# Context steps of two scan directions on the two halves of TensorE's columns, and the running tile of a triangular inverse in PSUM

## The chip, the cores and the metric

The kernel runs on one core of one Trainium2 chip. The metric is the device time of one execution in microseconds, as the median of several runs. The core has TensorE (PE in the rows, with its weight loads as PEld), VectorE (DVE), ScalarE (ACT), GpSimd (POOL), the SyncE queue that issues transfers (SP), SBUF, and PSUM with eight banks of 512 float32 per partition.

## The reference, cut to what matters

The program is a two-layer backbone over 256 latent tokens behind 256 context tokens, 1024 features wide. Layer 0 mixes time with a bidirectional RWKV-7 scan over 16 heads of 64 and then runs a mixture of experts; layer 1 is a short convolution and a second mixture of experts. The change touches the scan alone:

```python
def step(s, inp):
    w_t, k_t, v_t, kk_t, a_t, r_t = inp
    sa = jnp.einsum('bhvk,bhk->bhv', s, -kk_t)
    s = (s * w_t[:, :, None, :] + sa[..., None] * (kk_t * a_t)[:, :, None, :]
         + v_t[..., None] * k_t[:, :, None, :])
    y = jnp.einsum('bhvk,bhk->bhv', s, r_t) if with_output else None
    return s, y
...
for p, reverse in enumerate((False, True)):
    ...
    s_ctx, yc = _wkv_scan(dec_c, kd_c, v_c, kk_c, a_c, None, s0, reverse)
    _, yl = _wkv_scan(dec_l, kd_l, v_l, kk_l, a_l, r_l, s_ctx, reverse)
```

For each of the two directions the state runs first through the context, where only the state counts, and then through the latent tokens, where each step gives an output too.

## The kernel before

The scan is done in chunks of 64 tokens: four context chunks (group g = 0) and four latent ones (g = 1). Two heads make a block of 128 features, and eight blocks (`fb` 0 to 7) pass through a software pipeline. For each block the kernel does the following.

- `first`, `second` and `pre` make the operands of the chunks for each direction d: decays, keys, and the products `pab`, `pat` and `pq` on TensorE, which ScalarE and VectorE take out of PSUM.
- `inverse` inverts the unit triangular 32x32 blocks of all chunks of both directions by forward substitution on VectorE. After the transpose `a_l` there are 31 steps; each is a product `lv` from `a_l` and a column of the running tile `t_l` (L820), and a subtraction that updates `t_l` (L822). Then `t_l` is transposed into `t_d` (L824). Before each inverse GpSimd clears `t_l` and writes its unit diagonal (L809 and two `pcopy`).
- `solve` (per direction) copies `t_d` into the block diagonal `d_bd` on ScalarE (L831) and does six products per group on TensorE (L843). Their banks are those of the pool `p2pq`, four of them, which `pre` uses too. ScalarE takes three of the results out (L853, L858, L862), VectorE subtracts the last two from `rd` and `hk` (L869, L872). Two banks stay open as accumulators for a whole direction.
- `chain` runs the state through the eight chunks. A step (i, d) is a product with `hk` and `v_bd` (L886) and one with `rd` and the state `s_bd` (L893) into one bank `po` of a pool of two. In a context step only 64 rows of it are made. Then VectorE copies one head's state (L896) and ScalarE the other's (L897) back to SBUF for the next step. Latent steps also give 64 rows of output, which ScalarE copies (L901) or VectorE adds (L903).
- `finish` normalizes and gates the block's output.

The generators are interleaved by `drive`, which always advances the one that has used the smallest share of its weight; a scheduler then sets the final order of each engine's queue, and each engine works through its queue strictly in that order. For each block there are two drives: the first holds `solve` of the current block, 22 steps of the next block's inverse, `finish` of the previous block and `first` of the block after; the second holds `chain` of the current block (weight 16), the remaining steps of the inverse (11) and `both` (weight 22), which makes the operands of the block after. The last block has no inverse beside it: its `chain` and `finish` run in a third drive with high priority (weight 19), beside the output projection `project` of the first seven blocks. Four tiles of the pool `p2pq` then become the projection's accumulators.

## Time and profile before

| | us |
|---|---|
| median of 3 runs | 1366.07 (1361.18 to 1366.48) |
| the profiled execution | 1364.24 |
| its span in the profile | 1362.4 |
| busy in the span: PE, DVE, ACT, POOL | 1196.9, 763.2, 582.8, 235.4 |
| inverse, products `lv` (L820) and updates of `t_l` (L822), 248 each | 81.7 and 78.9 |

The span begins with the first instruction and ends with the last. The scan's pipeline takes up the time from about 160 to 640 us. An engine's busy share is an average over the span, so it is read stretch by stretch: the transposes L813 (start of an inverse) and L824 (its end) mark the blocks. A duration in brackets at the end of a row of the timeline is the engine's idle time before the row, with what ended it.

### The profile page before, as it was taken

To read this page: it belongs to the slowest core of one execution; us is meant where nothing else is said; L and a number is where in the kernel's file an instruction comes from. 1 tells how busy PE (TensorE), PEld (TensorE's weight loads), DVE (VectorE), ACT (ScalarE), POOL (GpSimd) and SP (SyncE) were. 2 spreads that over 40 slices of the span, in tenths; PEclk is the share of its full clock that TensorE was granted. 3 is DMA by queue.
4 is the path that set the end of the run, shared out by engine and by line. 5 is a ranking of instruction groups with operands and counts; after the bars stand their busy time and mean duration, and the time that the engine had idled before them with its cause. 6 is when DMAs were issued, how large, how long until landed. Compare 5 with 4: busy or idle time off the path is not lost. (4 is left out here: it accounts for less than half of the span.)

```text
span 1362.4 us, 22076 instructions
## 1 busy us (share of the span) xinstructions
PE 1196.9 (88%) x8560; PEld 845.6 (62%) x8560; DVE 763.2 (56%) x1855; ACT 582.8 (43%) x1187; POOL 235.4 (17%) x245
## 2 busy tenths in 40 slices
PE   2799888889989888899789999889898799999797
PEld 2588687777867777788744444334898734444344
DVE  5878888889989998875532121211677512121112
ACT  4667562666756757744312122212644312112113
POOL 3313443332231232100200000000523200000001
PEclk9999999999999999999889999989999899999898
DMA  9455634133322320137679999978653399999860
GB/s 355 177 178 172 211 109 124 59 121 115 96 90 83 96 82 25 64 138 315 227 295 418 420 420 419 419 296 324 214 186 129 119 376 419 419 420 420 326 245 31
DMA packets 64630, 311.76 MB, mean 229 GB/s; under 512 B 14464, under 2 KB 22912, under 8 KB 29696
## 3 DMA queue, kind: packets, MB, share of 16 engines
q1 hardware_dynamic: 60192, 303.59, 58.0%
q10 hardware_dynamic: 4320, 6.63, 1.4%
q8 instruction: 71, 1.16, 0.3%
q14 instruction: 47, 0.39, 0.1%
HBM read 301.80 MB, written 8.39 MB: 228 GB/s over the span
## 5 line engine op out<-in xcount | busy, mean ns | idle before, releaser
L1558 PE MATMUL wup<-w,xe 128*64 128x512 f32 (+1 forms) x1024 | 261.5, 612 | 5.8 <-DVEq L1724 5.8
L1563 DVE TENSOR_TENSOR sgate<-sgate,wup 64x512 f32<-64x512 f32 (+1 forms) x32 | 22.1, 690 | 250.1 <-ACT sgate L1562 227.6
L1558 PEld LDWEIGHTS wup<-w,xe 128*64 128x64 f32 (+1 forms) x1024 | 77.4, 142 | 129.6 <-issue 120.4
L1585 PE MATMUL y<-w,het 128*64 128x512 f32 (+1 forms) x512 | 127.7, 598 | 0.0
L1597 DVE SCALAR_TENSOR_TENSOR yy<-y,gw,yy 64x512 fp32r<-64x512 f32 (+1 forms) x64 | 48.0, 750 | 121.3 <-ACT yy L1596 121.0
L1562 ACT ACTIVATE sgate<-wup 64x512 f32<-64x512 f32 (+1 forms) x32 | 19.0, 593 | 181.6 <-PE wup L1558 181.6
L1596 ACT ACTIVATE yy<-y,gw 64x512 fp32r<-64x512 f32 (+1 forms) x64 | 43.8, 684 | 122.0 <-PE y L1585 106.5
L820 DVE TENSOR_TENSOR lv<-a_l,t_l 128x126 f32<-128x126 f32 (+22 forms) x248 | 81.7, 330 | 3.3
L822 DVE TENSOR_TENSOR t_l<-t_l,lv 128x126 f32<-128x126 f32 (+22 forms) x248 | 78.9, 318 | 3.4
L886 PE MATMUL po<-v_bd,hk 128*64 128x128 f32 (+1 forms) x256 | 56.6, 304 | 21.1 <-ACT s_bd L897 7.5
L1585 PEld LDWEIGHTS y<-w,het 128*64 128x64 f32 (+1 forms) x512 | 37.6, 140 | 60.5 <-issue 57.2
L1510 PEld LDWEIGHTS xeps<-g,h2t 128*128 128x128 f32 x256 | 37.5, 216 | 38.2 <-issue 21.3
L1510 PE MATMUL xeps<-g,h2t 128*128 128x256 f32 (+1 forms) x256 | 45.8, 321 | 17.2 <-DVE gw L1498 10.7
L1105 ACT CAST wh<-w 128x1024 fp32r<-128x1024 f32 x40 | 41.7, 1046 | 41.4 <-PE dps L143 24.3
L1771 POOL TENSOR_SCALAR idrw<-cst 128x1024 f32<-128x1024 f32 x2 | 5.5, 2770 | 303.0 <-PE acc L1605 274.0
L886 PEld LDWEIGHTS po<-v_bd,hk 128*64 128x64 f32 (+1 forms) x256 | 31.7, 163 | 41.3 <-ACT s_bd L897 14.4
L144 PE MATMUL dps<-xh,wl 128*128 128x258 f32 x192 | 55.2, 288 | 2.1 <-POOL wl L1108 2.1
L142 PE MATMUL dps<-xh,wh 128*128 128x258 f32 x192 | 55.5, 289 | 1.5 <-ACT wh L1105 1.5
L766 PE MATMUL pab<-bk,al_bd 128*128 128x128 f32 x256 | 40.4, 306 | 18.1 <-DVE bk L744 13.7
L722 POOL TENSOR_TENSOR al_bd<-kkh,peb 64x512 f32<-64x512 f32 x32 | 39.8, 1245 | 90.9 <-ACT peb L713 89.0
L1605 PE MATMUL acc<-st,yy 128*128 128x256 f32 x272 | 46.5, 305 | 10.3 <-PEq L1724 9.4
L143 PE MATMUL dps<-xl,wh 128*128 128x258 f32 x192 | 55.2, 287 | 0.0
(414 smaller groups left out, 2938.4 us busy)
## 6 DMA issues: line engine op xcount, KB each, us to landing
w<-in_wgu SPq DMA_DIRECT2D x128, 1024.0 KB, 9.6
w<-in_wd SPq DMA_DIRECT2D x64, 1024.0 KB, 9.4
w<-in_ada SPq DMA_DIRECT2D x46, 1024.0 KB, 6.5
w<-in_sc_in SPq DMA_DIRECT2D x12, 1024.0 KB, 5.0
w<-in_rk SPq DMA_DIRECT2D x8, 1024.0 KB, 5.3
w<-in_wv SPq DMA_DIRECT2D x4, 1024.0 KB, 5.8
w<-in_wo SPq DMA_DIRECT2D x4, 1024.0 KB, 9.3
w<-in_sc_out SPq DMA_DIRECT2D x4, 1024.0 KB, 5.2
```

Of the source, the lines that this page charges most:

```text
L142: mm(out, lhs[0], rhs[0], start=start, stop=False)
L143: mm(out, lhs[0], rhs[1], start=False, stop=False)
L144: mm(out, lhs[1], rhs[0], start=False, stop=stop)
L820: nc.vector.tensor_mul(u, a_l[:, kk:kk + 1, kk + 1:].broadcast_to([P, m, n]), t_l[:, 0:m, kk:kk + 1].broadcast_to([P, m, n]))
L822: nc.vector.tensor_sub(t_l[:, 0:m, kk + 1:], t_l[:, 0:m, kk + 1:], u)
L886: nc.tensor.matmul(po[d][i], q.hk[d][g][:, j], q.vbd[:, 4 * g + j], start=True, stop=i == 0)
L1510: nc.tensor.matmul(pt[:, f * m:f * m + m], h2t[k][:, t, fb * P:fb * P + P], g[:, t, :, :n], start=j == 0, stop=j == 3)
L1558: nc.tensor.matmul(gu[i], x(kc), w[:, 512 * i:512 * i + 512], start=kc == 0, stop=kc == NB - 1)
L1585: nc.tensor.matmul(ys[i], het[:, k], w[:, 512 * i:512 * i + 512], start=k == 0, stop=k == 3)
L1596: nc.scalar.activation(parts[i][0], ys[i], AF.Copy, scale=gws[i])
L1597: nc.vector.scalar_tensor_tensor(parts[i][1], ys[i], gws[i], parts[i][0].bitcast(F32), op0=ALU.mult, op1=ALU.subtract)
L1605: nc.tensor.matmul(acc[4 * i + q], part[:, q * P:q * P + P], st, start=first and q % 2 + k == 0, stop=last and k == len(y) - 1, skip_group ...
```

## The change

It has two parts, and two weights follow.

The running tile `t_l` moves from SBUF to a PSUM bank of its own (pool `p2pt`), and the pool `p2pq` of the products goes from four banks to three. GpSimd can no longer set the tile up, so a template `t_0` is made once in SBUF, and ScalarE copies it to `t_l` before each inverse, after the four copies into `a_d`. The projection's fourth accumulator is `t_l`'s bank.

In `chain` a context step does both directions at once: the two `hk` products, then the two `rd` products, into one bank, direction 0 in partitions 0 to 63 and direction 1 in 64 to 127. So direction 1's 64 weight columns lie on the other half of the array. The copies follow, direction by direction. Latent steps stay as they were, one direction at a time. A block's chain is 4 + 8 = 12 steps of `drive` in place of 16, and its weights go from 16 to 12 and from 19 to 15.

```diff
-            pq_ = es.enter_context(tc.tile_pool(name="p2pq", bufs=4, space=PSUM, **kw))
+            pq_ = es.enter_context(tc.tile_pool(name="p2pq", bufs=3, space=PSUM, **kw))
+            pst = es.enter_context(tc.tile_pool(name="p2pt", bufs=1, space=PSUM, **kw))
...
-            t_l = static([P, 16, 32], "t_l", None)
+            t_l = static([P, 16, 32], "t_l", None, pst)
+            t_0 = static([P, 16, 32], "t_0")
+            for a in range(2):
+                nc.gpsimd.tensor_scalar_mul(t_0.rearrange("p m r -> p (m r)")[:, a:a + 511:34],
+                                            self.k("unit", a, a + 1).broadcast_to([P, 16]), 1.0)
...
-                nc.gpsimd.memset(t_l, 0.0)
-                for a in range(2):
-                    pcopy(t_l.rearrange("p m r -> p (m r)")[:, a:a + 511:34],
-                          self.k("unit", a, a + 1).broadcast_to([P, 16]))
+                nc.scalar.copy(t_l, t_0)
...
-                for i in range(NCH):
-                    for d in range(2):
-                        g, j = where(i, d)
-                        hpart(i, d)
-                        p = po[d][i]
+                def step(i, ds):
+
+                    g = i // 4
+                    p = pc.tile([P, 512], F32, tag="pc", name="po")[:, :P]
+                    at = {d: (3 - i % 4 if d else i % 4, p if g else p[64 * d:64 * d + 64]) for d in ds}
+                    for d, (j, o) in at.items():
+                        nc.tensor.matmul(o, q.hk[d][g][:, j], q.vbd[:, 4 * g + j], start=True, stop=i == 0)
+                    for d, (j, o) in at.items():
                         if i > 0:
-                            nc.tensor.matmul(p, q.rd[d][g][:, j], s_bd[d][i % 2], start=False, stop=True)
+                            nc.tensor.matmul(o, q.rd[d][g][:, j], s_bd[d][i % 2], start=False, stop=True)
+                    for d, (j, o) in at.items():
                         if i < NCH - 1:
                             sn = s_bd[d][(i + 1) % 2]
-                            nc.vector.tensor_copy(sn[0:64, 0:64], p[0:64, 0:64])
-                            nc.scalar.copy(sn[64:, 64:], p[0:64, 64:])
+                            nc.vector.tensor_copy(sn[0:64, 0:64], o[0:64, 0:64])
+                            nc.scalar.copy(sn[64:, 64:], o[0:64, 64:])
...
+                for i in range(NCH):
+                    for ds in ((0,), (1,)) if i // 4 else ((0, 1),):
+                        step(i, ds)
                         yield
...
-                    drive((chain(cur), 16), (inv, 33 - SPLIT), (both(nn) if nn else None, 22),
+                    drive((chain(cur), 12), (inv, 33 - SPLIT), (both(nn) if nn else None, 22),
...
-            drive((urgent(seq(chain(prev), finish(prev)), 200), 19),
+            drive((urgent(seq(chain(prev), finish(prev)), 200), 15),
```

The queue of VectorE in the middle of a chain, for one block of the steady pipeline. `s_bd` are the state copies out of the chain's bank `po`, `lv` and `t_l` the inverse, `b_bd` a product of `pre` on its way out of `pab`; what an instruction waits for stands in brackets. Before:

```order
L896 COPY s_bd_2481<-po 64x64 [waits PE_49]
L820 TENSOR_TENSOR lv<-a_l,t_l 128x120 [waits DVE_49]
L896 COPY s_bd_2475<-po 64x64 [waits PE_49]
L822 TENSOR_TENSOR t_l<-t_l,lv 128x10x12 [waits DVE_49]
L752 TENSOR_TENSOR rd_2438<-rt,peb_1633 128x4x64 [waits Activation_49]
L820 TENSOR_TENSOR lv<-a_l,t_l 128x121 [waits DVE_49]
```

After:

```order
L893 COPY s_bd_2480<-po 64x64 [waits PE_49]
L824 TENSOR_TENSOR t_l<-t_l,lv 128x9x14 [waits DVE_49]
L709 TENSOR_SCALAR ws<-ws 128x512
L822 TENSOR_TENSOR lv<-a_l,t_l 128x130 [waits DVE_49]
L893 COPY s_bd_2484<-po 64x64 [waits Activation_49]
L824 TENSOR_TENSOR t_l<-t_l,lv 128x10x13 [waits DVE_49]
L711 SCALAR_TENSOR_TENSOR ls<-rst,ws 128x512
```

Direction 1's copy now waits for ScalarE, which reads direction 0's half of the same bank just before; and `ws` and `ls` of `first`, which stood ahead of the last subtractions of `solve`, now stand in the chain.

The same queue in the same block from the end of the inverse (`t_d`) to the start of the next (`a_l`). Before:

```order
L824 STREAM_TRANSPOSE t_d<-t_l 128x16x32 [waits DVE_49]
L896 COPY s_bd_2479<-po 64x64 [waits PE_49]
L896 COPY s_bd_2477<-po 64x64 [waits PE_49]
L774 TENSOR_TENSOR b_bd_1615<-pab,cst 64x4x64 [waits Activation_49]
L774 TENSOR_TENSOR b_bd_1615<-pab,cst 64x4x64
L903 TENSOR_TENSOR yt<-yt,po 64x128 [waits Activation_49]
L896 COPY s_bd_2481<-po 64x64 [waits PE_49]
L903 TENSOR_TENSOR yt<-yt,po 64x128 [waits Activation_49]
L799 TENSOR_TENSOR gq_1626<-pq,cst 128x512 [waits PE_49]
L796 TENSOR_TENSOR hk_2446<-pq,cst 128x4x64 [waits Activation_49]
L903 TENSOR_TENSOR yt<-yt,po 64x128 [waits PE_49] x2
L919 TENSOR_TENSOR yt<-yt,vt 128x256 [waits DVE_49]
```

After:

```order
L826 STREAM_TRANSPOSE t_d<-t_l 128x16x32 [waits DVE_49]
L779 TENSOR_TENSOR b_bd_1618<-pab,cst 64x4x64 [waits Activation_49]
L779 TENSOR_TENSOR b_bd_1618<-pab,cst 64x4x64
L893 COPY s_bd_2486<-po 64x64 [waits PE_49]
L804 TENSOR_TENSOR gq_1629<-pq,cst 128x512 [waits PE_49]
L900 TENSOR_TENSOR yt<-yt,po 64x128 [waits Activation_49]
L900 TENSOR_TENSOR yt<-yt,po 64x128 [waits PE_49] x2
L801 TENSOR_TENSOR hk_2451<-pq,cst 128x4x64 [waits Activation_49]
L919 TENSOR_TENSOR yt<-yt,vt 128x256 [waits DVE_49,Pool_49]
```

Two state copies and one output addition of the chain have moved ahead of the inverse's end.

TensorE's queue in the chain's context steps: `hk` and `rd` products of both directions beside the products `adaps` of another stage and `pab`, `pat` of `pre`. Before, an `hk` product and its `rd` product stood together and the `hk` product alone waited:

```order
L886 MATMUL po<-v_bd_2473,hk_1629 64x128 [waits Activation_49]
L893 MATMUL po<-s_bd_2481,rd_1621 64x128
L778 MATMUL pat<-cst,al_bd 128x128
L886 MATMUL po<-v_bd_2473,hk_1627 64x128 [waits Activation_49]
L893 MATMUL po<-s_bd_2475,rd_1619 64x128
```

After, the two `hk` products stand ahead, and each `rd` product waits for ScalarE by itself in the middle of other work:

```order
L771 MATMUL pab<-bk,al_bd 128x128 [waits DVE_49,Pool_49]
L771 MATMUL pab<-bk,al_bd 128x128 x3
L889 MATMUL po<-s_bd_2480,rd_2440 64x128 [waits Activation_49]
L783 MATMUL pat<-cst,al_bd 128x128 x4
L889 MATMUL po<-s_bd_2484,rd_2442 64x128 [waits Activation_49]
L886 MATMUL po<-v_bd_2476,hk_2448 64x128 [waits PE_49]
L886 MATMUL po<-v_bd_2476,hk_2450 64x128
```

What stands behind such an `rd` product on TensorE waits with it.

## Rows read from the trace of the kernel before

**Rows 1.** The page's line of the span, and VectorE's busy tenths in 40 slices.
```profile
span 1362.4 us, 22076 instructions
...
DVE  5878888889989998875532121211677512121112
```

**Rows 2.** Windows from L813 to `solve`'s end, six blocks: width, busy us, means.
```profile
sum 113.20, PE 105.86 PEld 99.14 DVE 107.99 ACT 75.96 POOL 18.72; mean PE 17.64 PEld 16.52 DVE 18.00 ACT 12.66 POOL 3.12
```

**Rows 3.** Windows from `solve`'s end to L824, five blocks; columns as in rows 2.
```profile
sum 128.50, PE 107.25 PEld 87.38 DVE 122.08 ACT 73.15 POOL 45.23; mean PE 21.45 PEld 17.48 DVE 24.42 ACT 14.63 POOL 9.05
```

**Rows 4.** Windows from L824 to the next L813, six blocks; columns as in rows 2.
```profile
sum 47.90, PE 41.20 PEld 37.12 DVE 30.03 ACT 45.27 POOL 6.08; mean PE 6.87 PEld 6.19 DVE 5.00 ACT 7.54 POOL 1.01
```

**Rows 5.** Groups by line, 307.6 to 570.5 us (five blocks): busy us, mean ns.
```profile
L820 DVE TENSOR_TENSOR lv<-a_l,t_l 128x56 f32<-128x56 f32 (+22 forms) x155 | 54.2, 350 | 1.3
L822 DVE TENSOR_TENSOR t_l<-t_l,lv 128x56 f32<-128x56 f32 (+22 forms) x155 | 52.8, 341 | 1.5
```

**Rows 6.** The two lines by themselves, whole span: ns min/median/max.
```profile
L820 DVE TENSOR_TENSOR lv<-a_l,t_l x248: 149/268/1349, 199.5 to 599.5; 128x126 f32<-128x126 f32 x12, 128x30 f32<-128x30 f32 x8, 128x56 f32<-128x56 f32 x8, 128x78 f32<-128x78 f32 x8
...
L822 DVE TENSOR_TENSOR t_l<-t_l,lv x248: 154/256/1362, 199.7 to 599.8; 128x126 f32<-128x126 f32 x12, 128x30 f32<-128x30 f32 x8, 128x56 f32<-128x56 f32 x8, 128x78 f32<-128x78 f32 x8
```

**Rows 7.** Timeline, GpSimd and VectorE: start us, duration us; two stretches of one block.
```profile
524.39 2.47 POOL L722 TENSOR_TENSOR al_bd<-kkh,peb 64x512 f32<-64x512 f32 x2 [11.22 <-ACT peb L713]
...
524.81 0.87 DVE L820 TENSOR_TENSOR lv<-a_l,t_l 128x56 f32<-128x56 f32 x1
525.71 0.35 DVE L869 TENSOR_TENSOR rd<-rd,pq 128x192 f32<-128x192 f32 x1
...
544.81 1.05 POOL L758 TENSOR_TENSOR bt<-bk,peb 128x512 f32<-128x512 f32 x1 [1.79 <-DVE bk L744]
544.85 0.21 DVE L896 COPY s_bd<-po 64x64 f32<-64x64 f32 x1
...
544.99 1.02 DVE L820 TENSOR_TENSOR lv<-a_l,t_l 128x130 f32<-128x130 f32 x1
```

**Rows 8.** Groups by line and shape, VectorE, 307.6 to 570.5 us.
```profile
L869 DVE TENSOR_TENSOR rd<-rd,pq 128x512 f32<-128x512 f32 x10 | 6.8, 680 | 0.0
L744 DVE TENSOR_TENSOR bk<-kd,ls 128x512 f32<-128x512 f32 x10 | 6.8, 678 | 0.0
L936 DVE TENSOR_SCALAR h<-pyt,vec 128x256 f32<-128x256 f32 x5 | 2.7, 539 | 0.0
L923 DVE TENSOR_TENSOR yt<-yt,mean 128x256 f32<-128x256 f32 x5 | 2.1, 420 | 0.0
```

**Rows 9.** Timeline, two output additions from partition 64 in a row.
```profile
569.48 0.61 DVE L903 TENSOR_TENSOR yt<-yt,po 64x128 f32<-64x128 f32 x2
```

**Rows 10.** Timeline of the last block's `solve`: products, and ScalarE's copy between.
```profile
605.42 1.00 PE L843 MATMUL pq<-kd,ao_bd 128*128 128x64 f32 x8
606.26 1.16 PE L843 MATMUL pq<-bk,ao_bd 128*128 128x128 f32 x8
...
606.47 0.38 ACT L858 ACTIVATE kd<-pq 128x256 f32<-128x256 f32 x1 [0.25 <-PE pq L843]
```

**Rows 11.** Timeline, one of `first`'s products in the middle of `solve`.
```profile
534.60 0.48 PE L691 MATMUL wp<-tw,l 128*128 128x512 f32 x1
```

**Rows 12.** ScalarE's state copies, 307.6 to 570.5 us; last, its idle time.
```profile
L897 ACT COPY s_bd<-po 64x64 f32<-64x64 f32 x70 | 14.1, 204 | 26.2 <-DVE s_bd L896 25.2
```

**Rows 13.** Waits of VectorE, 307.6 to 570.5 us: total us, times, longest us.
```profile
DVE b_bd L774 <- ACT apl L768: 6.1, 11, 1.0
DVE yt L903 <- ACT s_bd L897: 5.3, 5, 1.1
```

**Rows 14.** The last chain: issue of the projection's weights, and first latent step.
```profile
622.15 1.75 SPq L163 DMA_DIRECT2D w<-in_wo  x4
...
628.90 0.38 PE L886 MATMUL po<-v_bd,hk 128*128 128x128 f32 x1
```

**Rows 15.** The page's DMA issues: count, KB, us from issue to landing.
```profile
w<-in_wo SPq DMA_DIRECT2D x4, 1024.0 KB, 9.3
```

15 lines of the change are left out of this document (4 added, 11 removed).

## The prediction, written before the changed kernel ran

> **What bounds the kernel now.** I read the slices first: VectorE stands at seven to nine tenths from the fifth slice to the seventeenth, most of it the scan, and falls to one or two in the experts behind it [rows 1]. The profiled execution took 1364.24 us with a span of 1362.4 [rows 1], 1.8 below the median of 1366.07; the sum is made against the execution, and its difference is taken off the median.
>
> Then I cut a block of the scan into three stretches with the windows. **A** runs from the transpose L813 to the last subtraction of `solve`: six of them take 113.2 us, 18.9 each, with VectorE busy for 18.0 and TensorE for 17.6 [rows 2]. Both are full there. **B** runs from there to the end of the inverse, L824: five take 128.5, 25.7 each, VectorE 24.4, TensorE 21.5 [rows 3]. There VectorE is the bound and TensorE has 4 us to spare. **C** runs from L824 to the next L813: six take 47.9, 8.0 each, VectorE 5.0, TensorE 6.9, ScalarE 7.5 [rows 4]. That stretch is ScalarE's. Together a block takes 52.6 us. What a part of the change is worth depends on which stretch it falls in.
>
> **Part 1, the tile in PSUM.** Over five blocks L820 and L822 ran 155 times each with means of 350 and 341 ns [rows 5], while their medians are 268 and 256, with single ones of over 1300 [rows 6]. The timeline shows why. An L820 of 56 columns took 0.87 us while GpSimd's L722 ran, and one of 130 columns 1.02 us beside L758, whose end it outlasted by 0.15 [rows 7]. Between them L869, a longer instruction that takes one operand from PSUM, took 0.35 beside the same L722, and an L896 from PSUM 0.21 beside L758 [rows 7]. So on VectorE an instruction with both operands in SBUF is held up while GpSimd works, and one with an operand in PSUM isn't. With `t_l` in PSUM both lines have one operand there. By mean less median they lose 155 x 0.082 + 155 x 0.085 = 25.9 us in five blocks, 5.2 per block. Split by GpSimd's work, 3.1 us in A and 9.0 in B [rows 2, 3], 1.3 of them lie in A and 3.9 in B.
>
> In A the relief is worth little, since TensorE stays. In B I count three quarters, 3.0 us: behind the held-up instructions of the timeline stand mostly others with an operand in PSUM, and only now and then one, such as L744, that would be held up in their place. Bounds: 0 and 5.2 per block.
>
> Whether an instruction that writes PSUM is slower, no row shows, as VectorE writes no PSUM before. For reading, rows stand side by side: L869 with an operand in PSUM takes 680 ns for 512 columns, L744 with both in SBUF 678; but L936 out of PSUM takes 539 ns where L923 in SBUF takes 420 [rows 8], though it also reads two columns of scalars. So the price of a write lies between nothing, or a little less, and 0.12 us; I take nothing, as an update of `t_l` is most like L869. The Trainium skill speaks against this change here: "Perfetto Trace Analysis", section "Optimizing Scalar/DVE Operations", gives a VectorE instruction about 60 ns of fixed access time on SBUF and about 125 on PSUM, engine-busy time. By that page each of the 62 instructions of an inverse would cost 65 ns more, an estimate of 4 us per block, of which B's share would turn the sum into no gain; for reads, L869 and L744 [rows 8] contradict it.
>
> GpSimd's clearing of `t_l` goes and ScalarE's copy of `t_0` comes, 512 columns, by L858's 0.38 us for half as many at most 0.76 [rows 10]. It stands behind the copies into `a_d`, beside L813, and the first L820 waits for that transpose anyway. It can delay the first evacuations of `solve`: 0 to 0.76 us, I take 0.2, counted in A.
>
> **Three banks.** In `solve` two banks stay open, so one is left for what was done in two. Before, the product of `bk` with `ao_bd` started at 606.26, ahead of ScalarE's L858, which emptied its predecessor's bank from 606.47 to 606.85 [rows 10]. Now it has to wait for that: 0.6 us per direction, 1.2 per block, as TensorE has little else to do there. In exchange the order moves about three of `first`'s products (0.48 each [rows 11]) out of A: 1.5 less. A comes out at 1.2 + 0.2 - 1.5 = -0.1, and I take -0.5, since VectorE, whose queue loses work there, will stand ready at each subtraction.
>
> **What the order moves.** Counted over five blocks, VectorE has 58 to 65 instructions in A before and 52 after, 60 to 67 in B before and 71 to 78 after, 12 or 13 in C before and 7 to 11 after. So about nine leave A, where they cost nothing once TensorE is the bound, and twelve come to B, where each counts. By kind they are about five of the inverse, three state copies, two `b_bd` and two output additions, less one `kd`: at the inverse's 0.27 [rows 6], a copy's 0.21 [rows 7], 0.42 for 256 columns [rows 8], 0.30 [rows 9] and 0.68 for 512 [rows 8], that is 1.3 + 0.6 + 0.8 + 0.6 - 0.7 = 2.7, taken as 3.0. It eats the whole relief in B. Bounds: 2 and 4.
>
> **Part 2, the chain.** Its products and copies keep their number. Direction 1's state copies now read from partition 64, and direction 0's from 0. In the trace an L896 lets the next instruction start 0.14 us after its own start, long before its end [rows 7], while two output additions, which read from partition 64, follow each other at 0.3 us, their whole length [rows 9]. If the change of start partition is the reason, the four copies and the four instructions behind them lose some 0.1 each: 0 to 0.8 us per block, I take 0.5 in B. The Trainium skill has this as a rule: "VectorE: DVE Perf Modes", section "Two Vector instructions with no wait between them", says that an instruction starting on another quarter of the partitions than the last access to that memory waits for all earlier ones. By that page it is the upper end; rows 9 agree with it without proving it, since no state copy from partition 64 stands in the trace.
>
> Direction 1's copies also wait for ScalarE's copy of direction 0. Behind them on VectorE stands the inverse, and behind the `rd` products on TensorE stands `pre`. ScalarE's own state copies already waited 25.2 us in five blocks for VectorE's [rows 12], so the chain always was a relay; VectorE has three or four other instructions between the two copies, about 1 us, longer than the 0.2 of the copy [rows 12]. I take nothing, with up to 1 us per block as the bound. Two directions at once on the two halves of the array can save at most one of two products, which TensorE doesn't need in B.
>
> What does count is that the chain ends earlier. After L824 there remain two or three state copies and as many output additions less to two. In five blocks VectorE waited 5.3 us for ScalarE ahead of an output addition and 6.1 for `apl` [rows 13], a good part of it in C, and ScalarE, the bound there, loses four or five copies of 0.2 [rows 12]: I take -1.5 per block, bounds -0.5 and -2.5.
>
> **The last chain** stands alone behind `solve`. Its context steps run until 628.90, but the projection's weights are issued at 622.15 [rows 14] and land 9.3 us later [rows 15], so neither a quicker nor a slower context part is seen. The last `solve` pays its 1.2 us.
>
> **The sum.** Per block A -0.5, B -3.0 + 3.0 + 0.5 = +0.5, C -1.5, together -1.5; for seven blocks -10.5, with the last `solve` -9.3. On the median: 1366.07 - 9.3 = 1356.8, and I say **1356**.
>
> **The rivals.**
> *Relief whole.* The bound is VectorE throughout, and the order only moves its work about: then 5.2 per block come off, less the 0.5 of the overlap, 33 us in seven blocks, and the time is 1334. For it: VectorE is busy for 95% in A and B [rows 2, 3]. Against it: TensorE is as full in A. Chance 0.18.
> *Nothing gained.* `solve` sets A, and the chain's relay with its new waits sets B and C; VectorE's relief turns into waiting at L871, L874 and the state copies. Then the time is 1364 to 1366. Chance 0.19.
> *Three banks, slower.* `pre` too works through these banks, 14 products per block, and each holds its bank until ScalarE and, for `pab`, the second `b_bd` in VectorE's queue are through. If each starts 0.5 us later, that is 7 us per block against the 4.2 that TensorE has to spare in B [rows 3]; the rest, 2.8, is more than the forecast's 1.5, so +1.3 per block, and with the last `solve` 1376. It decides from 0.4 us per product (14 x 0.4 = 4.2 + 1.5). Chance 0.10.
> *Slow writes.* If an instruction on `t_l` costs 0.12 us more [rows 8] for the update alone, 18 of them in B on the path add 2.2 us per block, and the time is 1372. Against it stand L869 and L744 [rows 8]. The rule of "Perfetto Trace Analysis" on PSUM, named above from the Trainium skill, would lead here. Chance 0.08.
> That the halves of the array don't work at once is no rival of its own: nothing in the sum rests on it.
>
> **How the numbers follow.** The forecast has 0.45, with a range of its own from 1346 to 1364. A difference of 0.5% (6.8 us) is about what a measurement of this kernel can tell from no change, so faster means below 1359.2: the whole relief and seven tenths of the forecast, 0.18 + 0.32 = 0.50. Within: the rest of the forecast and most of the second rival, 0.13 + 0.18 = 0.31. Slower: 0.19 with the two last. The range goes from 1336, just above the whole relief, to 1371, and leaves out some 0.2, the outer halves of the first, third and fourth.
>
> **What would show it.** In the changed kernel's profile the means of L822 and L824 fall to their medians, about 0.27, and none lasts 0.8 us beside GpSimd; if they come out at 0.33 or more without GpSimd, writes are slow. Stretch A keeps its 18.4 us with VectorE idle for some 4 of them, waiting for `pq` at L871 and L874. B keeps about 26, C falls to 6.5. Long waits of `pab` and `pat` for VectorE or ScalarE would speak for the banks. The prediction is wrong if A shrinks with VectorE's work, or if B shrinks by more than 2 us.

## The result: 0.7% slower, and the profile after

The changed kernel took 1374.12 us in the median of 12 runs (1367.91 to 1376.94), the kernel before 1365.47 in 12 runs beside them. The ratio is 1.007, with a 95% interval from 1.0052 to 1.0088: slower, where 1356 was forecast. The profiled execution took 1374.96 us.

The page of the changed kernel (its span, VectorE's busy tenths in 40 slices, the granted clock of TensorE in tenths), and from the page of before the clock alone, which the prediction had not looked at:

```profile
span 1373.2 us, 22045 instructions
...
DVE  5879888788787888855442221111677512221112
...
PEclk8999999999999999978989999989999899999898
```
```profile
PEclk9999999999999999999889999989999899999898
```

The span is 10.8 us longer [rows 1]. VectorE has less to do, 733.7 us against 763.2, and the clock is lower at slices 18 and 19, the end of the scan. The windows of the changed kernel and of the kernel before, cut at the same two places, say where: a first row from the start of the second inverse to the start of the last, a second one from there to the last product on the state (width, busy us of each engine, granted clock, DMA share, GB/s):

```profile
257.20:566.80 309.60, 276.37 (x2476) 236.94 (x2476) 253.94 (x802) 212.40 (x491) 77.41 (x83) 0.97 0.26 84
566.80:651.00 84.20, 74.79 (x611) 65.23 (x611) 49.05 (x159) 33.43 (x87) 3.38 (x2) 0.84 0.41 150
```
```profile
257.30:570.50 313.20, 275.10 (x2482) 238.85 (x2480) 283.72 (x802) 210.18 (x487) 83.78 (x101) 0.98 0.25 83
570.50:636.80 66.30, 61.46 (x583) 55.56 (x584) 48.62 (x160) 31.70 (x86) 3.39 (x2) 1.00 0.47 172
```

Over six periods the changed kernel gains 3.6 us, though VectorE works 29.8 us less in them. Behind that it takes 17.9 more: 10.5 in the last inverse (30.8 to 41.3 us, up to the end of its transpose), 4.7 in the last `solve` (21.4 to 26.1), 2.8 in the last chain up to its last product on the state (14.1 to 16.9). These 2.8 do not reach the time: the last product of the projection, which runs beside this chain and behind it, ends 47.6 us after the last `solve` before and 47.5 after. So the last inverse and the last `solve` are the loss. In the second row TensorE's granted clock is 0.84 against 1.00. It has two levels, 2.4 GHz (1.0) and 1.2 GHz (0.5), so it stood at the lower one for a third of that stretch.

The relief itself came as forecast. The two lines of the inverse in the changed kernel, 306.5 to 566.8 us (busy us, mean ns), and each by itself over the span (ns min/median/max):

```profile
L824 DVE TENSOR_TENSOR t_l<-t_l,lv 128x56 f32<-128x56 f32 (+22 forms) x155 | 39.2, 253 | 1.5
L822 DVE TENSOR_TENSOR lv<-a_l,t_l 128x56 f32<-128x56 f32 (+22 forms) x155 | 37.5, 242 | 1.5
...
L822 DVE TENSOR_TENSOR lv<-a_l,t_l x248: 131/252/297, 200.2 to 606.2; 128x126 f32<-128x126 f32 x12, 128x30 f32<-128x30 f32 x8, 128x56 f32<-128x56 f32 x8, 128x78 f32<-128x78 f32 x8
...
L824 DVE TENSOR_TENSOR t_l<-t_l,lv x248: 174/264/306, 200.4 to 606.6; 128x126 f32<-128x126 f32 x12, 128x30 f32<-128x30 f32 x8, 128x56 f32<-128x56 f32 x8, 128x78 f32<-128x78 f32 x8
```

The means fell from 350 and 341 ns [rows 5] to 242 and 253, and nothing lasts over 306 ns, where single ones had lasted 1349 and 1362 [rows 6]. The update that now writes PSUM has a median of 264 ns against 256 in SBUF; shape by shape, the fastest instruction of each of the 23 shapes is longer by 11 ns in the median.

For the stretches I have to mend my own windows first: those of rows 2 and 3 ended A 2.6 to 4.2 us ahead of the last subtraction of `solve`, so that B had a piece of A. Cut at that subtraction's end, five blocks each, A, B and C of the kernel before and then of the changed one (sum of widths, busy us, means):

```profile
sum 111.90, PE 103.29 PEld 93.82 DVE 108.14 ACT 74.79 POOL 23.32; mean PE 20.66 PEld 18.76 DVE 21.63 ACT 14.96 POOL 4.66
...
sum 116.50, PE 97.54 PEld 80.06 DVE 110.30 ACT 70.23 POOL 40.63; mean PE 19.51 PEld 16.01 DVE 22.06 ACT 14.05 POOL 8.13
...
sum 34.50, PE 29.20 PEld 26.72 DVE 19.77 ACT 33.00 POOL 5.07; mean PE 5.84 PEld 5.34 DVE 3.95 ACT 6.60 POOL 1.01
```
```profile
sum 105.60, PE 103.92 PEld 95.33 DVE 87.12 ACT 68.20 POOL 21.52; mean PE 20.78 PEld 19.07 DVE 17.43 ACT 13.64 POOL 4.30
...
sum 134.40, PE 111.94 PEld 89.96 DVE 111.28 ACT 92.31 POOL 43.02; mean PE 22.39 PEld 17.99 DVE 22.26 ACT 18.46 POOL 8.60
...
sum 20.30, PE 14.90 PEld 12.79 DVE 14.62 ACT 19.58 POOL 0.00; mean PE 2.98 PEld 2.56 DVE 2.92 ACT 3.92 POOL 0.00
```

Per block A goes from 22.4 to 21.1, C from 6.9 to 4.1, B from 23.3 to 26.9. In B VectorE's work is what it was, 110.3 and 111.3; its idle time went from 6.2 to 23.1 us. The waits of VectorE in the changed kernel, 310 to 570 us (total us, times, longest us), name the wait:

```profile
DVE s_bd L893 <- PE po L889: 14.3, 15, 3.4
```

In the kernel before, the same state copy waited 3.1 us in that stretch, less than the two waits of rows 13:

```profile
DVE s_bd L896 <- PE po L893: 3.1, 5, 0.8
```

Block by block, B takes 28.6, 25.2, 30.3, 25.2 and 25.1 us after, and 23.2, 23.3, 24.7, 23.3 and 22.0 before. Most of the growth lies in the first and the third of these, in which TensorE stood still for 1.71 us (at 331) and 2.25 us (at 437) for a weight of the modulation, line L186, that had not landed.

### The profile page after: what moved, and what is told of

Read it like the earlier page. It is cut to its first block, busy times and chain, and to the rows that moved or that the text cites. A ratio compares the mean times of both kernels' runs of the same rounds, so it can differ in the third digit from the quotient of the medians.

```text
span 1373.2 us, 22045 instructions
## 1 busy us (share of the span) xinstructions
PE 1204.5 (88%) x8560; PEld 846.7 (62%) x8560; DVE 733.7 (53%) x1855; ACT 586.6 (43%) x1195; POOL 227.6 (17%) x224
## 5 line engine op out<-in xcount | busy, mean ns | idle before, releaser
L1564 DVE TENSOR_TENSOR sgate<-sgate,wup 64x512 f32<-64x512 f32 (+1 forms) x32 | 22.1, 690 | 250.1 <-ACT sgate L1563 227.7
L1597 ACT ACTIVATE yy<-y,gw 64x512 fp32r<-64x512 f32 (+1 forms) x64 | 43.7, 682 | 122.1 <-PE y L1586 106.6
L824 DVE TENSOR_TENSOR t_l<-t_l,lv 128x126 f32<-128x126 f32 (+22 forms) x248 | 63.1, 254 | 3.2
L822 DVE TENSOR_TENSOR lv<-a_l,t_l 128x126 f32<-128x126 f32 (+22 forms) x248 | 60.5, 244 | 3.5
L1511 PEld LDWEIGHTS xeps<-g,h2t 128*128 128x128 f32 x256 | 36.8, 213 | 38.2 <-issue 21.3
L1511 PE MATMUL xeps<-g,h2t 128*128 128x256 f32 (+1 forms) x256 | 45.1, 317 | 17.2 <-DVE gw L1499 10.7
L186 PE MATMUL adaps<-w,sc 128*32 128x128 f32 x1216 | 52.6, 292 | 6.4 <-DMA w<-in_ada 4.0
L886 PE MATMUL po<-v_bd,hk 128*64 128x128 f32 (+1 forms) x256 | 50.2, 305 | 5.9 <-ACT yt L898 4.9
```

The costliest lines, as they stand in the source:

```text
L186: nc.tensor.matmul(ps[32 * j:32 * j + 32, :], self.sc[:, 2 * kc:2 * kc + 32], w[:, P * j:P * j + P], start=kc == 0, stop=kc == NB - 1)
L822: nc.vector.tensor_mul(u, a_l[:, kk:kk + 1, kk + 1:].broadcast_to([P, m, n]), t_l[:, 0:m, kk:kk + 1].broadcast_to([P, m, n]))
L824: nc.vector.tensor_sub(t_l[:, 0:m, kk + 1:], t_l[:, 0:m, kk + 1:], u)
L886: nc.tensor.matmul(o, q.hk[d][g][:, j], q.vbd[:, 4 * g + j], start=True, stop=i == 0)
L1511: nc.tensor.matmul(pt[:, f * m:f * m + m], h2t[k][:, t, fb * P:fb * P + P], g[:, t, :, :n], start=j == 0, stop=j == 3)
```

## The experiments

Letters say what a kernel starts from: p1 is part 1 alone, p2 part 2 alone, b the kernel before, a the changed one. Each was timed beside the kernel before (its medians: 1365.5, 1363.5, 1365.3, 1365.1, 1364.1 and 1362.6 us in the six sets of runs), and the ratio is to that. "Six periods" is from the start of the second inverse to that of the last; "behind solve" is the part of the last inverse behind the last subtraction of the block ahead, and its number of instructions on VectorE; the stretches are of the one profiled execution, us. How much chance is in a stretch shows where an edit does not reach: the six periods are 309.6 us in the changed kernel and 306.7 in a_fill, whose edit lies behind them. Kernels whose medians differ by up to some 4 us have intervals that overlap.

| kernel | median us | ratio (95%) | six periods | last inverse | behind solve | last solve |
|---|---|---|---|---|---|---|
| before | 1365.5 | | 313.2 | 30.8 | 11.8 (45) | 21.4 |
| after | 1374.1 | 1.007 (1.0052 to 1.0088) | 309.6 | 41.3 | 21.1 (65) | 26.1 |
| p1_tile | 1365.7 | 1.0005 (0.998 to 1.0029) | 302.0 | 39.5 | 17.5 (65) | 27.6 |
| p2_steps | 1367.1 | 1.0013 (0.9986 to 1.0041) | 307.8 | 34.0 | 15.0 (45) | 21.4 |
| b3_banks | 1369.5 | 1.0037 (1.0016 to 1.0059) | 317.9 | 31.4 | 11.5 (44) | 22.2 |
| a_old67 | 1370.8 | 1.0046 (1.0027 to 1.0064) | 309.4 | 36.8 | 16.7 (62) | 23.7 |
| p1_inv | 1363.2 | 0.9997 (0.9978 to 1.0017) | 303.7 | 37.2 | 13.2 (47) | 21.9 |
| a_inv | 1371.6 | 1.0054 (1.0033 to 1.0075) | 310.2 | 44.2 | 16.2 (44) | 21.9 |
| b_inv | 1367.8 | 1.0024 (1.0009 to 1.0039) | 310.7 | 31.4 | 8.8 (39) | 24.2 |
| a_w16 | 1373.3 | 1.0082 (1.0052 to 1.0111) | 304.3 | 43.7 | 15.6 (49) | 24.7 |
| a_fill | 1370.0 | 1.0045 (1.0027 to 1.0063) | 306.7 | 42.5 | 22.4 (62) | 21.9 |
| a_dep | 1371.1 | 1.005 (1.0031 to 1.0069) | 308.5 | 41.3 | 16.9 (58) | 24.3 |
| p1_dep | 1361.1 | 0.9967 (0.9953 to 0.998) | 299.8 | 36.6 | 16.2 (58) | 23.5 |
| p2_fat | 1365.5 | 0.9998 (0.9981 to 1.0015) | 307.8 | 32.3 | 13.1 (45) | 22.1 |
| a_ada | 1373.3 | 1.0071 (1.0046 to 1.0095) | 305.3 | 44.1 | 19.8 (68) | 23.8 |
| a_all | 1370.2 | 1.0045 (1.0028 to 1.0063) | 306.9 | 40.2 | 20.0 (64) | 21.8 |
| p1_depfill | 1361.4 | 0.9983 (0.9965 to 1.0002) | 300.4 | 36.6 | 16.1 (55) | 22.9 |
| a_alldep | 1369.3 | 1.0043 (1.0021 to 1.0065) | 310.5 | 38.7 | 18.6 (56) | 22.8 |
| b_late | 1365.5 | 1.0011 (0.999 to 1.0032) | 312.4 | 30.7 | 11.7 (46) | 25.0 |
| b_late2 | 1372.4 | 1.007 (1.0045 to 1.0094) | 312.9 | 30.7 | 11.7 (46) | 30.7 |

**First group: the parts apart.** p1_tile has the diff's first part, p2_steps its second, b3_banks only the pool's size, a_old67 the old steps in the last two blocks:

```
p1_tile:  def chain as before; (chain(cur), 16), ... 19)
p2_steps: t_l in SBUF, p2pq bufs=4; def chain as after; 12, 15
b3_banks: -p2pq bufs=4   +p2pq bufs=3, and a bank that only project uses
a_old67:  +(chain_o(cur), 16) if fb == NB - 2 else (chain(cur), 12); chain_o(prev), 19
```

> Part 1 alone: the running tile of the inverse in PSUM, three banks for the products, ScalarE's copy of the start tile; the context steps and the two weights are those of the kernel before. Theory 'last chain': the 0.7% come from the context steps beside the last inverse, where TensorE stands at 1.2 GHz and waits; with the old steps the last inverse (from the transpose of a_l to that of t_d) takes about 30 us as before and not 40, the gain that the scan had collected by there (3.7 us) stays, less about 1 us in the last solve: 1361 to 1364 us. Theory 'three banks': TensorE's wait of 0.5 us for ScalarE's copy in each of 16 solve halves, and like waits in the block's preparation, cost 7 us or more, hidden nowhere: 1371 to 1375 us. Theory 'relief is the whole gain': the shorter L822 and L824 show in full where the relay of the context steps is not tied to them: below 1350 us.

> Part 2 alone: context steps of both directions together on the two halves of the array, with the weights 12 and 15; the running tile stays in SBUF with GpSimd's clearing, and four banks stay for the products. Theory 'last chain': the last inverse takes about 40 us, the granted clock falls to 0.5 to 0.7 in it, as in the changed kernel, and no relief pays for it elsewhere: 1374 to 1382 us. Theory 'three banks': without that wait the kernel is no slower than before, 1360 to 1366 us. Theory 'relief is the whole gain of the scan': the period of a block is that of before, 52.2 us, or a little above.

> The kernel before with three banks instead of four for the products of solve and of the block's preparation, and nothing else. Theory 'last chain': each solve half shows one wait of 0.5 us more on TensorE, of which the blocks in the middle hide most: 1365 to 1369 us. Theory 'three banks': 1371 to 1376 us, and the last inverse or the last solve longer by several us.

> The changed kernel with the old form of the context steps, one direction after the other on all rows, and the old weights 16 and 19, in the last two blocks alone (the one beside the last inverse and the one behind it). Theory 'last chain': the first six blocks keep their gain, 51.6 us a period, the last inverse takes about 30 us and the last solve 22 to 23: 1360 to 1364 us. Theory 'three banks': no change against the changed kernel, 1372 to 1375 us, with the last solve still at 26 us.

Each part alone is as fast as before, and none of the theories had both ("three banks" had it of p2_steps, about a microsecond lower). b3_banks is slower than before by 0.37%. a_old67 came between its two theories. Part 1 gains 11.2 us in six periods, and against b3_banks, which has its three banks, 15.9, or 2.7 per block: the relief. It loses 8.7 in the last inverse and 6.2 in the last `solve`, with the old context steps, so "last chain" fell as it stood. The fewer banks by themselves cost 4.7 us in six periods and 0.8 in the last `solve`. Part 2 gains 5.4 in six periods and loses 3.2 in the last inverse. Together they should gain some 16 there; they gain 3.6.

TensorE in p1_tile at the end of the last inverse (start, duration, name, count, and in brackets the idle time and who ended it):

```profile
599.82 0.69 PE L934 MATMUL pyt<-cst,yt 128*128 128x128 f32 x2 [4.54 <-DVE yt L930]
...
601.24 3.78 PE L845 MATMUL pq<-gq,d_bd 128*128 128x64 f32 x16
```

The same in the changed kernel, up to where the products have their old length again:

```profile
608.65 0.69 PE L932 MATMUL pyt<-cst,yt 128*128 128x128 f32 x2 [4.75 <-DVE yt L928]
...
610.07 3.78 PE L845 MATMUL pq<-gq,d_bd 128*128 128x64 f32 x16
613.64 1.81 PE L845 MATMUL pq<-kd,ao_bd 128*128 128x64 f32 x8
615.92 2.07 PE L845 MATMUL pq<-bk,ao_bd 128*128 128x128 f32 x8 [0.47 <-ACT kd L860]
...
619.39 1.32 PE L845 MATMUL pq<-bk,d_bd 128*128 128x128 f32 x8
620.54 0.78 PE L845 MATMUL pq<-kd,at_bd 128*128 128x64 f32 x6
```

In the kernel before the last `solve` started right behind the last product on the state:

```profile
603.25 0.39 PE L893 MATMUL po<-s_bd,rd 128*128 128x128 f32 x2
603.54 2.05 PE L843 MATMUL pq<-gq,d_bd 128*128 128x64 f32 x16
```

Two things are to be seen. TensorE waits 4.5 to 4.8 us for the end of block 6 (`finish`), which now stands ahead of the last `solve` in its queue. And behind that gap it runs at half speed: the 16 instructions of `gq` (each product counts as two) take 3.78 us, with the clock up 1.95 to 2.05, eight of `kd` 1.81 in place of 1.00 [rows 10]. The windows of the changed kernel show the clock over that stretch, and an earlier fall beside the last but one block's context steps (at 601 to 606 us it is 1.00):

```profile
591.00:596.00 5.00, 4.61 (x33) 2.63 (x30) 2.93 (x13) 1.29 (x6) 0.00 (x0) 0.65 0.69 293
596.00:601.00 5.00, 5.00 (x40) 3.65 (x39) 1.73 (x9) 1.37 (x6) 0.00 (x0) 0.67 0.11 20
...
606.00:611.00 5.00, 2.35 (x9) 1.75 (x9) 3.50 (x10) 2.13 (x5) 0.00 (x0) 0.52 0.42 165
611.00:616.00 5.00, 4.53 (x22) 4.34 (x21) 0.00 (x0) 1.34 (x3) 0.00 (x0) 0.50 0.00 0
```

The two falls part by kernel. The one in 591 to 601 us is in the kernels with joint steps beside the last inverse (after, p2_steps) and not in before, b3_banks, p1_tile or a_old67. It does not come each time: of the later kernels with these steps a_fill and a_inv have it, while a_dep, a_w16 and a_ada do not, and a_dep has the same two gaps in the steps as the changed kernel, 0.59 and 0.33 us. The one ahead of the last `solve` is in those with the tile in PSUM (after, p1_tile, a_old67) and not in before, b3_banks or p2_steps. Why the tile brings it, VectorE's rows say, of the kernel before and then of the changed one:

```profile
599.75 0.19 DVE L822 TENSOR_TENSOR t_l<-t_l,lv 128x16 f32<-128x16 f32 x1
...
600.30 1.04 DVE L824 STREAM_TRANSPOSE t_d<-t_l 128x512 f32<-128x512 f32 x1
...
604.05 0.43 DVE L919 TENSOR_TENSOR yt<-yt,vt 128x256 f32<-128x256 f32 x1
```
```profile
604.67 0.42 DVE L919 TENSOR_TENSOR yt<-yt,vt 128x256 f32<-128x256 f32 x1
...
606.63 0.17 DVE L824 TENSOR_TENSOR t_l<-t_l,lv 128x16 f32<-128x16 f32 x1
606.75 0.42 DVE L925 TENSOR_REDUCE mean<-vt 128x4 f32<-128x256 f32 x1
607.09 1.03 DVE L826 STREAM_TRANSPOSE t_d<-t_l 128x512 f32<-128x512 f32 x1
```

Before, the inverse was through and transposed ahead of the first row of `finish`, L919. In the new order the rows of `finish` stand one by one between the last pairs of the inverse: 65 instructions behind `solve` in place of 45. In the whole last inverse VectorE is busy for 30.6 us in place of 27.0, and idle for 10.7 in place of 3.8: about a third of the 10.5 us is work that has moved in, the rest is waiting.

**Second group: the order.** The last inverse is put ahead in the order, in part 1, in the changed kernel and in the kernel before; a_w16 has the old weights.

```
+if fb == NB - 2:
+    inv = urgent(inv, 200)
...
a_w16: (chain(cur), 16), ... 19)
```

> Part 1 alone (tile in PSUM, three banks, old context steps), and the last inverse, the one beside the context steps of the last but one block, put ahead in the order: its rows no longer stand alternately with those of the context steps and of the block's end in VectorE's queue. Theory 'order': part 1 had gained 11 us by the last inverse and lost 15 behind it, since VectorE took the block's end ahead of the inverse's transpose and TensorE stood 4.5 us idle and then worked at a granted clock of 0.5. With the order mended the last inverse takes about 31 us instead of 39.5, the last solve 22 to 23 at full clock instead of 27.6: 1351 to 1357 us. Theory 'three banks': the last solve is slow for its bank waits, whatever the order: 1362 to 1366 us. Theory 'clock by itself': the clock falls there whatever stands ahead of solve: 1360 to 1366 us.

> The changed kernel with the last inverse put ahead in the order, and nothing else. Theory 'order': the stretch of 41 us from the transpose of a_l to that of t_d shrinks to 31 to 34 us (the context steps of both directions may still pull the clock down, 3 us in part 2 alone), the last solve to 22 to 23 us: 1360 to 1366 us. Theory 'context steps': the loss is in the steps, and the time stays at 1371 to 1375 us.

> The kernel before with its last inverse put ahead in the order. Theory 'order': there the transpose of t_d already stands ahead of the block's end on VectorE, so that nothing is to be mended: 1362 to 1367 us, the last inverse at 29 to 31 us. If the mending is worth something by itself, whatever the tile: 1357 us or less.

> The changed kernel with the old weights 16 and 19 for the context steps in place of 12 and 15, so that a step of both directions at once comes as often in the order as a step of one did. Theory 'relay': VectorE's state copies wait for TensorE's products on the state (14 us from 310 to 555 us, against 2.4 before), since both directions' products stand between the preparation's in TensorE's queue, and the weights only place them; the waits stay at 10 us or more, the period at 51 to 52 us, and the time at 1368 to 1375 us. Theory 'weights': with the steps sooner the waits fall to less than 5 us, the period to 50 us, as in part 1 alone: 1358 to 1366 us.

The last `solve` came to 21.9 us in p1_inv and a_inv, as "order" said, but the lift also moved work in the blocks ahead: in p1_inv the clock fell from 511.9 on behind a gap of 1.6 us, in a_inv from 570.6 behind one of 3.1. So p1_inv only equals the kernel before, and a_inv's 2.5 us less are within the intervals; both times lie where the rivals of "order" had them. b_inv is slower than before by 0.24%: the lift is worth nothing there. In a_w16 the waits at L893 fell to 6.4 us and the six periods by 5.3, near what "weights" said of them, but the time stayed within the intervals: the last inverse took 43.7 us, with the clock down from 563 behind a gap of 3.0. So the weights place those waits, and the loss at the end has another cause.

**Third group: idle time and the clock.** a_fill puts 20 useless products into the 4.75 us gap. a_dep and p1_dep make the end of block 6 wait for the last transpose. p2_fat runs the products of the joint steps beside the last inverse three times.

```
a_fill, last context step of block 6:
+for _ in range(20):
+    nc.tensor.matmul(pf, q.hk[0][1][:, 0], q.vbd[:, 4], start=True, stop=True)
...
a_dep, p1_dep, in finish of block 6:
+nc.gpsimd.tensor_scalar_mul(t4, t_d[:, 31, 0:4], 0.0)
+nc.gpsimd.tensor_add(bn, bn, t4)
...
p2_fat, joint steps of block 6:
+for _ in range(2):
+    nc.tensor.matmul(o, q.hk[d][g][:, j], q.vbd[:, 4 * g + j], start=True, stop=True)
```

> The changed kernel with 20 products of no use (one product of the last but one block's context repeated into a bank of its own, which nobody reads) put into TensorE's queue where it stood idle for 4.75 us, between the last context step beside the last inverse and the transposes of that block's end. Work is added and nothing is moved. Theory 'clock': the fall of the granted clock from 606 to 620 us comes from that idle time; with TensorE busy it stays at 1.0 there, the first products of the last solve take 2.05 us and not 3.78, the last solve 21.5 to 23 us instead of 26.1, and the time falls by 3 to 6 us: 1367 to 1371. Theory 'order alone': the clock there is a matter of chance or of the program's place, the products cost what they cost, 0 to 4 us: 1374 to 1378 us.

> The changed kernel, in which the end of the last but one block waits for the last inverse's transpose (its sum over heads gets zero times four elements of it, two small instructions on GpSimd). So VectorE has the inverse's last four pairs ahead of that block's end, and TensorE the first products of solve ahead of its transposes; all else is in the place of the changed kernel. Theory 'order': the 4.75 us of idle time ahead of solve shrink to 2 us or less, the last inverse loses 2 to 3 of its 41 us and the last solve comes to 22 us at full clock: 1363 to 1368 us. If the clock falls all the same, since some idle time is left: 1369 to 1373 us.

> The same dependence in part 1 alone (tile in PSUM and three banks, old context steps, old weights). Theory 'order': up to the last inverse nothing moves, so the 11 us gained by there stay, and of the 15 us lost behind it 8 to 11 come back: 1354 to 1359 us, faster than both kernels. If idle time and a fall of the clock remain ahead of the last solve: 1361 to 1365 us.

> Part 2 alone (context steps of both directions at once, tile in SBUF, four banks), and in the four joint steps beside the last inverse each product with v_bd runs three times instead of once, to no use, so that TensorE is busier there. Theory 'clock': in part 2 the clock fell to 0.5 from 593 to 600 us, behind three gaps of 0.3 to 0.6 us in these steps; with more work in them it stays at 1.0, and the last inverse takes 31 to 33 us and not 34: 1363 to 1367 us. If the clock falls there for another reason, the added 1.8 us (16 products at 0.22 us, two at a time) come on top: 1367 to 1371 us, with 34 us or more for the last inverse.

a_fill has more work, and its median is 4.1 us lower, as "clock" said; its interval still overlaps that of the changed kernel (1.0027 to 1.0063 against 1.0052 to 1.0088), so the gain in time is at the edge of what can be told. The rows are clear. TensorE's in it, where the 20 products show as 40 instructions:

```profile
603.12 4.64 PE L908 MATMUL pf<-v_bd,hk 128*128 128x128 f32 x40
...
609.58 2.05 PE L845 MATMUL pq<-gq,d_bd 128*128 128x64 f32 x16 [0.33 <-ACT d_bd L833]
...
612.94 1.16 PE L845 MATMUL pq<-bk,ao_bd 128*128 128x128 f32 x8 [0.47 <-ACT kd L860]
```

The useless products end where the wait had ended, `gq` takes 2.05 us again, and the last `solve` 21.9 instead of 26.1. p2_fat asks the same of the joint steps. Windows of p2_steps and of p2_fat:

```profile
592.00:596.00 4.00, 3.67 (x20) 2.44 (x21) 2.73 (x13) 1.09 (x5) 0.00 (x0) 0.63 0.65 272
596.00:600.00 4.00, 4.00 (x28) 2.97 (x27) 1.56 (x9) 0.93 (x4) 0.00 (x0) 0.52 0.02 4
```
```profile
592.00:596.00 4.00, 3.47 (x41) 2.41 (x41) 3.26 (x16) 0.82 (x4) 0.61 (x1) 1.00 0.80 336
596.00:600.00 4.00, 4.00 (x40) 2.66 (x32) 2.79 (x14) 1.86 (x8) 0.00 (x0) 1.00 0.00 0
```

With three times the products the clock stays up and the last inverse takes 32.3 us, not 34.0; on the time that is 1.6 us, within the intervals. a_all and a_alldep, further down, have the threefold products too and no fall there; but without them three kernels of seven had none either, so that the products keep the clock up is likely and not shown. p1_dep beats both kernels: 1361.1 us, faster than before by 0.33% (0.2 to 0.47). It keeps part 1's six periods, and the last `solve` falls from 27.6 to 23.5. A gap of 4.67 us is left there, so it came to the upper branch of what was expected:

```profile
597.75 3.57 PE L845 MATMUL pq<-gq,d_bd 128*128 128x64 f32 x16 [4.67 <-ACT d_bd L833]
```

TensorE no longer waits for the end of block 6 there but for the inverse itself, which ScalarE copies into `d_bd`; in a_old67 too a gap of 5.03 us ends with `d_bd`. So the place of `finish` is only part of it: the last inverse comes late. a_dep's median is 3.0 us lower, within the intervals, with its gap still at 4.89.

**Fourth group: the pieces together.** a_ada puts the modulation's products (L186) behind most of the context steps; a_all adds a_fill and the useless products of p2_fat to it; a_alldep adds a_dep to that; p1_depfill is p1_dep with the 20 useless products.

```
-(adas(ADA2[fb]), ADA2[fb]))
+(late(8, adas(ADA2[fb])), 10))
```

> The changed kernel with the modulation's products (L186) that stand beside the context steps put behind eight tenths of that stretch in the order instead of ahead of it. Theory 'idle time, then clock': in blocks 1 and 3 TensorE stood 1.7 and 2.3 us at L186 for a weight that had not landed, with the context steps' products queued behind it, VectorE waited up to 3.4 us for those at L893, and the clock fell behind both (333 and 439 us); with L186 later all three go, and the period of these blocks comes to 50 to 51 us: 1367 to 1371 us. Theory 'relay': VectorE's waits at L893 come from the joint steps in TensorE's queue and stay at 12 us or more from 310 to 555 us; the time stays at 1372 to 1376 us.

> The changed kernel with three of these edits together: the modulation's products later, each product of the four joint steps beside the last inverse run three times, and the 20 products of no use in the idle time ahead of the last solve. Theory 'idle time, then clock': the scan of the changed kernel lost 15 us more of TensorE's full speed to the lower clock than the kernel before (23.7 against 8.5 us); without the falls at 333, 439, 592 and 606 us some 12 of them are back, and the time is 1360 to 1366 us although 36 products are added. Theory 'order alone': each edit brings what it brought alone or nothing, and the added work costs: 1368 to 1374 us.

> Part 1 alone with the end of the last but one block behind the last inverse's transpose (the fastest so far), and the 20 products of no use in the 4.7 us in which TensorE still stood idle ahead of the last solve. Theory 'idle time, then clock': the fall from 598 to 601 us goes, the last solve takes 21.9 us instead of 23.5: 1358 to 1361 us. If the filling costs more than it saves: 1361 to 1365 us.

> The changed kernel with the three edits against idle time (modulation's products later, joint steps beside the last inverse with threefold products, 20 products ahead of the last solve), and besides the end of the last but one block behind the last inverse's transpose. With the three alone the clock in the scan was nearly that of the kernel before (6.8 us of full speed lost against 5.1, counted from the second block's inverse on), and still the last inverse took 40 us against 31 and its second part had 64 instructions on VectorE against 45. Theory 'order': what is left of the loss is this row of VectorE's; with seven of them behind the transpose the last inverse takes 33 to 37 us: 1364 to 1368 us. Theory 'relay': the joint steps' waits set that stretch, it stays at 39 to 41 us: 1369 to 1372 us.

What a_ada was to mend stood in the changed kernel in block 3, TensorE's rows and then VectorE's:

```profile
439.50 0.61 PE L186 MATMUL adaps<-w,sc 128*32 128x128 f32 x2 [2.25 <-DMA w<-in_ada]
...
441.62 0.69 PE L889 MATMUL po<-s_bd,rd 128*64 128x128 f32 x2
```
```profile
445.13 0.22 DVE L893 COPY s_bd<-po 64x64 f32<-64x64 f32 x1 [3.37 <-PE po L889]
```

The wait for the weight and the falls behind it are gone, VectorE's waits at L893 went from 14.3 to 7.9 us (310 to 555 us), and the six periods shrank by 4.3 us. But the last inverse grew by 2.8, other gaps opened ahead of the last `solve`, and the time stayed. a_all and a_alldep missed their 1360 to 1368 and came where "order alone" and "relay" had them: the clock falls nowhere in the last inverse of either, and it still takes 40.2 and 38.7 us. So of the changed kernel's loss the clock is a part. What is left is in VectorE's queue there, but the joint steps are only some of it: in a_alldep the state copies wait 3.9 us in the last inverse, before 1.1, and p1_dep, without joint steps and at full clock until the inverse ends, takes 36.6 us as well. p1_depfill came 0.4 us above p1_dep: the fall behind its gap is gone, and nothing is gained that can be measured.

**Fifth group: the converse.** The kernel before, with its last `solve` made to wait for the end of block 6. The end of block 6 is written ahead of that `solve` in both. b_late put the wait on the part of `t_d` that the second direction reads, which held nothing up; b_late2 puts it on the first.

```
+nc.scalar.copy(t4, q.after[:, 0, 0:4])
+nc.gpsimd.tensor_scalar_mul(t4, t4, 0.0)
+nc.gpsimd.tensor_add(t_d[:, 31, 0:4], t_d[:, 31, 0:4], t4)
...
b_late2: t_d[:, 0, 0:4]
```

> The kernel before with one wait added: the last solve starts behind the end of the last but one block (zero times four elements of that block's normed output is added to four elements of t_d), so that TensorE, which worked without a break there, stands idle for some 5 to 6 us. Theory 'idle time, then clock': the wait costs its 5 to 7 us, and besides the granted clock falls behind it and the first direction of the last solve takes 4 to 5 us more at half speed: 1374 to 1378 us, with gq's 16 products at 3.8 us instead of 2.05. If idle time has no such price: 1369 to 1372 us.

> As b_late, but with the added wait on the part of t_d that the first direction of the last solve reads (b_late had put it on the second direction's, where it held nothing up: TensorE stood idle for 0.9 us there and not for 5). Now TensorE's queue has the block's end and half of the modulation's products ahead of solve, and it stands idle for some 6 us. Theory 'idle time, then clock': against b_late the wait costs 5 to 7 us, and behind it the granted clock is 0.5 for much of the first direction, whose 16 products of gq take 3.8 us and not 2.05: 1373 to 1378 us, and the last solve with the idle time 33 us or more. If idle time has no price beyond its own length: 1369 to 1372 us, with gq at 2.05 us.

b_late says little, as its wait did not bind, though its last `solve` takes 25.0 us: the clock falls at 600.8 behind gaps of 0.81 and 0.86 us. b_late2 took 1372.4 us, 6.9 more than b_late, between the ranges of the two theories. Its rows:

```profile
606.95 0.69 PE L937 MATMUL pyt<-cst,yt 128*128 128x128 f32 x2 [3.93 <-DVE yt L933]
...
609.67 1.97 PE L848 MATMUL pq<-gq,d_bd 128*128 128x64 f32 x8 [0.61 <-ACT d_bd L836]
611.57 3.37 PE L186 MATMUL adaps<-w,sc 128*32 128x128 f32 x62
```

The gap pulls the clock down in the kernel before too: eight instructions of `gq` take 1.97 us, which take 1.10 at full clock (a_alldep, 610.01), and the 62 of L186 take 3.37 where 64 take 1.95 in b_late. That is 2.3 us on those rows, beside 4.5 us of the gaps themselves. The sign is as expected; the price is about half of what I had put.

## Why the prediction was wrong, step by step

**The relief** was right: 3.0 us per block counted, 2.7 measured between b3_banks and p1_tile. Writing PSUM costs an update 8 ns in the median, so the rival of slow writes is out. The Trainium skill's rule against this part ("Perfetto Trace Analysis", "Optimizing Scalar/DVE Operations") does not hold here: by its 60 and 125 ns it would have been some 65, an estimate.

**Three banks** were right in size: a wait of 0.47 us where 0.6 was taken, and 4.7 us in six periods, 0.8 per block against 1.2. **The copies from partition 64** were too: L893 lets the next instruction start after 0.14 us out of partition 0 and after 0.25 out of 64 (445.13 to 445.27, 446.10 to 446.35). The trace agrees with the rule of the Trainium skill that I had named for it ("VectorE: DVE Perf Modes", "Two Vector instructions with no wait between them").

**A and C** did better than forecast, -1.3 and -2.8 per block against -0.5 and -1.5. VectorE's idle time in A, 18.5 us in five blocks, is the 4 per block that was to be seen.

**B failed**, +3.6 against +0.5. The step was "I take nothing, with up to 1 us per block as the bound" for the relay of the joint steps. I had priced what VectorE does in B, and there it has 0.2 us per block more to do, where the sum had +0.5. I had not priced what it waits for: the wait at the state copies grew from 3.1 to 14.3 us, 2.2 per block. The order rows ahead of the prediction showed the place, a product on the state behind those of `pab`; what they could not show is the wait of 2.25 us for a weight that came ahead of these. Neither part alone has this wait: from 310 to 555 us it is 14.3 us in the changed kernel, 2.4 before, 4.8 in p1_tile and 0.5 in p2_steps. a_w16 and a_ada, which only move rows, halve it, to 6.4 and 7.9; so it is the order's at least as much as the joint steps'. Why just both parts together give this order is open.

**The last inverse and the last `solve` failed most.** "The last `solve` pays its 1.2 us" took the eighth inverse for one like the others. But there `finish` of block 6 comes into VectorE's queue among the inverse, the inverse ends late, and TensorE, with no block behind, has nothing to fill the gap. 10.5 + 4.7 us went there, most of the 18 us between the forecast's -9.3 and the +8.7 measured.

**The clock** had no term at all. From the second inverse to the last product on the state the changed kernel lost 22 us of TensorE's full speed to the lower level, the kernel before 5 (half of each stretch at 1.2 GHz). Not all of it is time: a_all lost 6.8 and still took 1370.2 us. In the last `solve` the fall cost 4.2 us (26.1 against 21.9 in a_fill); the falls in the middle follow gaps of 1.4 to 2.3 us.

The rival "three banks, slower" named 1376, close to the result, by a mechanism that the runs reject as the main one: b3_banks takes 1369.5. That a quicker or slower context part of the last chain is not seen in the time was right: the last chain took 2.8 us more, at 1.2 GHz from 637 to 644, and the projection ended no later behind the last `solve`. One slip is in the first rival: 1366.07 less 33 is 1333, not 1334.

## What to carry to other kernels

An engine that is made quicker brings its rows closer to the engine it waits for, and the gaps move there. Where TensorE is near full, price a gap of several microseconds at its length and reckon with half speed behind it, and look for gaps at the pipeline's last block, where nothing fills them. When an operand changes its memory, read the whole new order, and above all which rows of other stages now stand between those of the critical one.

## What the runs showed of the hardware

The granted clock of TensorE fell to half behind every gap of 3.7 to 5.0 us in the scans of these kernels, and behind some of the shorter ones: behind 2.25 us at 437 in the changed kernel, and not behind 1.97 at 564 in the same trace or 3.16 at 571 in b_inv. Which of the short ones it follows is open. Work of no use in the gap of 4.75 us kept it up (a_fill). Products of 0.27 us that use the two halves of the columns by turns start 0.05 to 0.06 us behind each other (p2_fat, 589.71, 589.77, 589.82), where on one half they start 0.11 behind each other (before, 590.86 and 590.97). VectorE writes PSUM nearly as fast as SBUF here (264 against 256 ns), and with one operand in PSUM none of 496 instructions was held up (at most 306 ns), though 136 of them ran while GpSimd did; before, 61 outlasted the shortest of their shape by over 0.15 us, all of them while GpSimd ran.
